# Taps in DRAM by lag then row, a modulation chunk in another place, and eight final stores of 32 rows

## The chip, the cores and the metric

The kernel runs on one core of a Trainium2 chip. The metric is the device time of one execution in microseconds (us), the median of several runs. The engines are PE (TensorE: matmuls; its weight loads are listed as PEld), DVE (VectorE), ACT (ScalarE), POOL (GpSimd) and SP (SyncE, which here only issues DMAs). DMAs are issued from the queues of SP, ACT and POOL and are carried by 16 DMA engines.

## What is computed

Two layers of a diffusion backbone over 256 latent tokens and 256 context tokens, width 1024. Layer 0 mixes tokens with a bidirectional diagonal state space (S5, 64 groups of 16 channels, 64 states per group) and a gated linear unit (GLU), then a dense SwiGLU. Layer 1 is grouped-query attention and a top-2-of-8 expert SwiGLU. Every sub-layer is modulated by vectors that come from one wide product:

```python
def _modulation(cvec, w, b):
    return jnp.split(jax.nn.silu(cvec) @ w + b, N_MOD, axis=-1)     # w: (1024, 6 * 1024) per layer

def _s5_mixer(hl, hc, ...):
    for r in range(2):                                              # forward, reverse
        sc_re, sc_im = _s5_scan(u_c, ..., None, reverse)            # context
        fin = last state of the context
        sl_re, sl_im = _s5_scan(u_l, ..., fin, reverse)             # latent, starts from it
        y_l = y_l + _s5_readout(sl_re, sl_im, c_re[r], c_im[r])
        y_c = y_c + _s5_readout(sc_re, sc_im, c_re[r], c_im[r])
    ...
# layer:  xl = xl + ml[2] * mixer(...);  xl = xl + ml[5] * ffn(...)
```

The output is the latent stream, 256 x 1024 float32.

## The kernel before

**State space part.** The 512 tokens are cut into 64 blocks of 8 tokens (32 context, 32 latent). Within a block the state space is a short convolution whose kernel (the *taps*: 15 lags, -7 to 7, a 16 x 16 matrix for each of the 64 groups) is worked out on the chip; between blocks a recurrence over 63 steps carries the states (*the scan*, `scan_range`, three DVE instructions a step, lines 844, 847, 849).

**Main loop.** 18 rounds (`for i in range(n + 2)`), three stages deep: `z_mul` (products on DVE, line 574, in some rounds sums, line 579), `z_tr` (transposes on PE, line 588, evicted by ACT, line 589), `v_stage` (PE lines 654 and 655) and `t_stage` (PE line 667, evicted by ACT into `VS`, lines 670 and 673). Work of `w_gen` (DVE, lines 680 to 702) fills gaps. At the end of the loop the order of DVE, ACT and PE is pinned to the order in which the code is written.

**Modulation chunks.** `ada_todo` is a list of 20 chunks of 512 columns, (0,4) to (0,11) and then (1,0) to (1,11), always taken in that order. For a chunk, two loads of 1 MB go out on SP; `ada_go` does 16 matmuls (line 264) and an eviction (line 270); `ada_done` does four transposes (line 284) and an eviction into `part` (line 285). With the last chunk of a group, which is (0,11), (1,3) or (1,11), two DVE instructions follow that sum `part` into `cols` (lines 289 and 291). Before the change the chunks go like this: (0,4) to (0,10) in the seven rounds named by `FILL`; (0,11) and (1,0), named `two`, within the taps, after `taps(1)` and after `taps(2)`; (1,1) and (1,2) after the two halves of the context read-out; and (1,3) in the `while` behind it, which runs until 8 are left. Loads use a rotation of four 1 MB buffers, `raw`.

**Taps and windows.** `taps(q)`, q from 0 to 3, works out a quarter of the taps on PE (lines 771 and 776) with ACT building the weights (line 755), and writes it to a DRAM tensor `Kd` by six DMAs on SP (lines 782 to 784). `windows(blk, hf)` reads a quarter back as a block Toeplitz matrix, 128 rows x 2048 values, 1 MB, on SP (line 791): row (a, l) of it holds the taps of lags a to a + 7 for channel l. `inner` multiplies it with the tokens (PE line 804) into eight `pz` banks. Then `states` copies scan states (ACT line 858; line 875 is the place of its call that the trace names), `outer` multiplies them in (PE line 866), and `gelu` evicts. The context half (h = 0) needs scan steps 1 to 31; the latent half (h = 1) needs all of them and follows the end of the scan. After it the GLU starts (PE line 1027).

In the stretch of the taps, the order of ACT, PE and SP is pinned to the written order. The order of DVE is not: there the tile planner, which works with costs of its own, decides where the two instructions of a `cols` sum stand among the scan's.

**End.** After the last expert, `finish` adds its result to `acc` in four DVE instructions (line 1992), and `store` sends each quarter of the output (128 rows of tokens, half of the columns) to DRAM on SP (line 2048).

Of the kernel before, what the change touches and what calls it, by code (L numbers as in the profile page):

```python
# [10 lines left out]
F32 = mybir.dt.float32  # L11
# [11 lines left out]
G, P, I = 64, 64, 16  # L23
# [20 lines left out]
AT = (15, 6, 4, 6, 6, 7, 25, 26, 26, 26, 28, 28, 29, 29, 29, 29, 30, 30, 33, 33, 33, 33, 34, 35, 35, 35, 35, 35, 35, 36)  # L44
RAW3 = 2
WOP = ((13, 13, 17, 17, 18, 19, 20, 20, 21, 21, 22, 22, 24, 24, 24, 24), (29, 29, 30, 30, 31, 32, 33, 34, 35, 35, 36, 36))
FILL = (3, 5, 6, 7, 10, 11, 13)
LATE = 8
ZSUM = (4, 5, 6, 8, 10, 13, 15)
WN = (0, 6, 1, 2, 1, 1, 2, 2, 2, 2, 1, 4, 2, 1)  # L50
# [29 lines left out]
def backbone_kernel(ctx: ExitStack, tc: tile.TileContext, x, c, cx, c_ctx, ada_w, ada_b, norm_mix_g, norm_ffn_g,  # L80
# [212 lines left out]
    def ada_next(n):  # L293
        return [ada_load(*ada_todo.pop(0)) for _ in range(min(n, len(ada_todo)))]
# [9 lines left out]
    def ada_done():  # L304
        while ada_open:
            ada_turn(*ada_open.pop(0))
# [17 lines left out]
    for r in range(2):  # L324
        src = bn[:, r].rearrange("g r (p i) -> g (r p) i", i=I)
        for q in range(2):
            t = ps()
# [269 lines left out]
    t = ps()  # L597
    T.transpose(t[:, :128], pr, ident)
    S.activation(pcol, t[:, :128], AF.Copy)
    t = ps()  # L600
# [141 lines left out]
        pass  # L742


    Kd = dram.tile([4, I, 15, 16 * I], F32, name="Kd")
    bd = [[wk.tile([128, 4, 64], F32, name=f"bd{r}{b}") for r in range(2)] for b in range(2)]
    for b in range(2):
        for r in range(2):
# [2 lines left out]
    def bd_fill(n_):  # L751
        for r in range(2):
            for d in range(2):
                rs = slice(64 * d, 64 * d + 64)
                S.activation(bd[n_ % 2][r][rs, :, 16 * d:48].rearrange("p g (o i) -> p g o i", i=16)[:, :, 0:3 - d:2 - d, :],
                             BB[r][rs, 4 * n_:4 * n_ + 4, None, :].to_broadcast([64, 4, 2, 16]), AF.Copy)

    def taps(q):

        ks = wk.tile([128, 9, 8, I], F32, name="ks", bufs=2)  # L760
        for q4 in range(4):
            n_ = 4 * q + q4
            if n_ + 1 < 16:
                bd_fill(n_ + 1)
            t = ps()
            tv = t[:, :288].rearrange("p (g s i) -> p g s i", g=2, s=9)
            for j in range(2):
                for r in range(2):
                    for zz in range(2):
                        gl = 2 * j + zz  # L770
                        T.matmul(t[64 * zz:64 * zz + 64, 144 * j:144 * j + 144], lhsT=bd[n_ % 2][r][:, gl, :],  # L771
                                 rhs=W[q // 2][r][:, (4 * n_ + gl) % 32].rearrange("p s i -> p (s i)"),
                                 start=(r == 0), stop=False)
                for zz in range(2):
                    rs = slice(64 * zz + 32, 64 * zz + 48)
                    T.matmul(t[64 * zz:64 * zz + 64, 144 * j:144 * j + 16], lhsT=ident[rs, 64 * zz:64 * zz + 64],
                             rhs=dm[rs, 2 * n_ + j, :], start=False, stop=True)
            S.activation(ks[:, :, 2 * q4:2 * q4 + 2, :].rearrange("p s g i -> p g s i"), tv, AF.Copy)
        for zz in range(2):
            kv = Kd[q, :, :, 128 * zz:128 * zz + 128]  # L780
            k_ = ks.rearrange("p s g i -> p s (g i)")
            SY.dma_start(kv[:, 8:15], k_[64 * zz:64 * zz + 16, 1:8])
            SY.dma_start(kv[:, 0:7], k_[64 * zz + 16:64 * zz + 32, 2:9])
            SY.dma_start(kv[:, 7], k_[64 * zz + 32:64 * zz + 48, 0])
# [3 lines left out]
    def windows(blk, hf):  # L788
        M = Mt[blk, hf] = raw_tile([8, 16 * I])
        k_ = Kd[2 * blk + hf]  # L790
        SY.dma_start(M.rearrange("p t k -> p (t k)"),
                     bass.AP(tensor=k_.tensor, offset=k_.offset, ap=[[16 * I, 8], [15 * 16 * I, 16], [1, 8 * 16 * I]]))

    def outs(pz, hf):
        for b in range(4):
# [9 lines left out]
                     start=(gl < 4), stop=False)  # L805

    two = [ada_next(1)[0] for _ in range(2)]
    bd_fill(0)
    pz = {}
    for q in range(4):  # L810
        taps(q)
        if q == 1:
            for hf in range(2):
                windows(0, hf)
            ada_done()
            ada_go(two[0])
        elif q == 2:
            ada_done()
            ada_go(two[1])
    for hf in range(2):  # L820
        windows(1, hf)
    ada_done()
# [1220 lines left out]

    ov = out[0].rearrange("(c b t) d -> b t c d", b=2, t=4)

    def store(lt, n):
        ns = slice(512 * n, 512 * n + 512)
        SY.dma_start(ov[lt, :, :, ns], acc[:, lt, ns])

    def finish():  # L2050

        e_ = NE - 1
        y = mp.tile([128, 512], F32, name="y0", tag="y0")
        for n in range(2):
            rs_n = slice(64 * n, 64 * n + 64)
            V.tensor_tensor(y[rs_n, :], yps[e_][0][rs_n, :], grow[0][rs_n, 512 * n:512 * n + 512], op=OP.mult)
        for lt, n, t in spread(e_, y):
            add(e_, lt, n, t)
            store(lt, n)

    def chain(*gens):
        for g in gens:
# [52 lines left out]
    with tc.If(nmax > 128):  # L2115
        op_, op_cm = popen("op", 1, "right")
        for e_ in range(NE):
            se = op_.tile([128, 2, 128], F32, name="se")
            pz = op_.tile([128, 2], F32, name="pz")
            V.tensor_scalar(pz, pos[:, :, e_], capv[:, e_:e_ + 1], None, op0=OP.subtract)  # L2120
            hf = op_.tile([128, 2, D], F32, name="hf")
            for lt in range(2):
                V.tensor_scalar(se[:, lt, :], iota, pz[:, lt:lt + 1], None, op0=OP.is_equal)
                V.tensor_tensor(hf[:, lt, :], h2[0][:, lt, :].bitcast(F32), h2[1][:, lt, :].bitcast(F32), op=OP.add)
            xg = op_.tile([128, KT, 128], F32, name="xg")
            for q in range(2):
                t = ps()
                for j in range(4):
                    for lt in range(2):
                        T.matmul(t[:, 128 * j:128 * j + 128],  # L2130
                                 lhsT=hf[:, lt, 512 * q + 128 * j:512 * q + 128 * j + 128], rhs=se[:, lt, :],
                                 start=(lt == 0), stop=(lt == 1))
                S.activation(xg[:, 4 * q:4 * q + 4, :].rearrange("p a b -> p (a b)"), t, AF.Copy)
            yp = [ps("py") for _ in range(2)]
            for f in range(DFF // 256):
                t = ps()
                for half in range(2):
                    w = load(moe_gu[0, e_].rearrange("(k p) n -> p k n", p=128)[:, :, DFF * half + 256 * f:
                                                                                  DFF * half + 256 * f + 256], [KT, 256])
                    for kt in range(KT):  # L2140
                        T.matmul(t[:, 256 * half:256 * half + 256], lhsT=xg[:, kt, :], rhs=w[:, kt, :],
                                 start=(kt == 0), stop=(kt == KT - 1))
                a = op_.tile([128, 256], F32, name="a")
                S.activation(a, t[:, 0:256], AF.Silu)
                V.tensor_tensor(a, a, t[:, 256:512], op=OP.mult)
                t = ps()
                for j in range(2):
                    T.transpose(t[:, 128 * j:128 * j + 128], a[:, 128 * j:128 * j + 128], ident)
                aT = op_.tile([128, 256], F32, name="aT")
                S.activation(aT, t[:, 0:256], AF.Copy)  # L2150
                w = load(moe_dn[0, e_][256 * f:256 * f + 256, :].rearrange("(k p) n -> p k n", p=128), [2, D])
                for j in range(2):
                    for n in range(2):
                        T.matmul(yp[n], lhsT=aT[:, 128 * j:128 * j + 128], rhs=w[:, j, 512 * n:512 * n + 512],
                                 start=(f == 0 and j == 0), stop=(f == DFF // 256 - 1 and j == 1))
            so = op_.tile([128, 256], F32, name="so")
            t = ps()
            for lt in range(2):
                T.transpose(t[:, 128 * lt:128 * lt + 128], se[:, lt, :], ident)
            S.activation(so, t[:, 0:256], AF.Copy)  # L2160
            for n in range(2):
                y, u = [op_.tile([128, 512], F32, name=t_) for t_ in ("y", "u")]
                S.activation(y, yp[n], AF.Copy)
                for lt in range(2):
                    t = ps()
                    T.matmul(t, lhsT=so[:, 128 * lt:128 * lt + 128], rhs=y, start=True, stop=True)
                    av = acc[:, lt, 512 * n:512 * n + 512]
                    V.scalar_tensor_tensor(u, t, gates[:, lt, e_:e_ + 1], grow[0][:, 512 * n:512 * n + 512], op0=OP.mult, op1=OP.mult)
                    V.tensor_tensor(av, av, u, op=OP.add)
        for n in range(2):  # L2170
            for lt in range(2):
                store(lt, n)
        pclose(op_cm)


# [28 lines left out]
```

## Time and profile before

| what | value |
|---|---|
| median of 3 runs | 1636.08 us (1635.64 to 1639.44) |
| profiled execution: its own time | 1639.6 us |
| profiled execution: span of the trace | 1637.8 us |
| PE busy | 1493.1 us (91%) |
| DVE busy | 891.7 us (54%) |
| ACT busy | 705.7 us (43%) |
| DMA queue of SP | 392.13 MB, 65.9% of 16 engines |

How to read it: the shares are means over stages with different limits. From about 940 us to the end the 16 DMA engines are full with expert weights; from about 270 to 940 us PE is nearly full; ahead of that stands the state space part, where PE, DVE and the DMA engines each have long gaps. [...] All times in the rows below are counted from the start of the span.

### The profile page before, as it was taken

The numbers are of one execution on the slowest core, as the hardware profiler recorded it, in microseconds if no ns is written. First come the engines' busy times: TensorE is split into PE (matmuls) and PEld (weight loads), VectorE is DVE, ScalarE is ACT, GpSimd is POOL, SyncE is SP. The second block draws the span as 40 slices with busy tenths as digits, with TensorE's granted clock in tenths as the row PEclk, the third lists the DMA queues.
The fourth block names the chain that finished last, engine by engine and source line by source line (L and its number), as shares of the span: only waits on it lengthen the run. The fifth ranks groups of instructions, "written<-read, shape, count | busy, mean of one in ns | idle before, by whom it ended". The sixth has DMA issues, their size and how long they took to land.

```text
span 1637.8 us, 24181 instructions
## 1 busy us (share of the span) xinstructions
PE 1493.1 (91%) x9790; PEld 1055.9 (64%) x9790; DVE 891.7 (54%) x1385; ACT 705.7 (43%) x930; POOL 38.3 (2%) x69
## 2 busy tenths in 40 slices
PE   4898656999999999999899899989999999989994
PEld 3555446876888888878767778437853685367631
DVE  6996568336333343335786777327831785168611
ACT  4687355325221221224585566226721673056400
POOL 1001000000000000001001000000000000000020
PEclk9996777999999999999999899999999999999998
DMA  9672585426332332235441579999999999999994
GB/s 264 229 261 60 108 209 171 156 81 218 107 102 77 103 103 84 97 103 158 172 164 48 205 254 360 387 403 409 405 406 402 408 405 405 404 408 405 395 405 192
DMA packets 163720, 398.48 MB, mean 243 GB/s; under 512 B 11964, under 2 KB 62336, under 8 KB 162960
## 3 DMA queue, kind: packets, MB, share of 16 engines
q1 hardware_dynamic: 161408, 392.13, 65.9%
q0 software_dynamic: 1184, 3.18, 0.8%
q10 hardware_dynamic: 1008, 1.55, 0.4%
q8 instruction: 79, 1.29, 0.3%
q14 instruction: 41, 0.34, 0.1%
HBM read 394.78 MB, written 2.05 MB: 242 GB/s over the span
## 4 chain that ended last, share of the span: by engine, by line
PE 77%; DMA 8%; DVE 5%; ACT 4%; issue 1%; SPq 0%; ACTq 0%; DVEq 0%
PE pgu L971 10%; PE pgu L970 10%; PE pgu L972 10%; PE pgu L1921 8%; DMA raw<-in_moe_w_gate_up_dram 3%; DMA raw<-Kd 3%; PE pd L970 3%; PE pd L972 3%; PE pd L971 3%; PE py L970 2%; PE py L971 2%; PE py L1984 2%; PE py L972 2%; PE ada L264 1%; PE ps L771 1%; DMA raw<-in_moe_w_down_dram 1%
## 5 line engine op out<-in xcount | busy, mean ns | idle before, releaser
L951 DVE TENSOR_TENSOR lo<-raw,hi 128x2048 fp32r<-128x2048 f32 (+1 forms) x184 | 401.1, 2187 | 215.5 <-ACT hi L951 214.6
L951 ACT ACTIVATE hi<-raw 128x2048 fp32r<-128x2048 f32 (+1 forms) x184 | 337.4, 1834 | 323.8 <-PE pd L971 81.1
L1921 PE MATMUL pgu<-raw,xb 128*32 128x512 f32 (+1 forms) x1536 | 157.0, 558 | 2.2 <-DMA raw<-in_moe_w_gate_up_dram 2.2
L970 PE MATMUL pgu<-hi,xa 128*128 128x512 f32 (+1 forms) x384 | 148.4, 386 | 5.3 <-ACT hi L951 5.3
L971 PE MATMUL pgu<-lo,xa 128*128 128x512 f32 (+1 forms) x384 | 147.2, 383 | 5.5 <-DVE lo L951 5.5
L972 PE MATMUL pgu<-hi,xa 128*128 128x512 f32 (+1 forms) x384 | 146.0, 380 | 0.0
L970 PE MATMUL pgu<-hhi,hi 128*128 128x512 f32 x352 | 137.0, 390 | 0.5 <-ACT hhi L1102 0.5
L971 PE MATMUL pgu<-hlo,hi 128*128 128x512 f32 x352 | 137.1, 390 | 0.0
L972 PE MATMUL pgu<-hhi,lo 128*128 128x512 f32 x352 | 137.0, 389 | 0.0
L1921 PEld LDWEIGHTS pgu<-raw,xb 128*32 128x32 f32 x1536 | 48.4, 110 | 98.7 <-issue 86.6
L970 PEld LDWEIGHTS pgu<-hi,xa 128*128 128x128 f32 x384 | 74.5, 194 | 23.7 <-ACT hi L951 6.0
L971 PEld LDWEIGHTS pgu<-lo,xa 128*128 128x128 f32 x384 | 74.6, 194 | 19.1 <-DVE lo L951 6.4
L1984 PE MATMUL py<-raw,aT 128*32 128x512 f32 x704 | 80.3, 594 | 6.4 <-DMA raw<-in_moe_w_down_dram 6.2
L972 PEld LDWEIGHTS pgu<-hi,xa 128*128 128x128 f32 x384 | 74.4, 194 | 13.8
L970 PEld LDWEIGHTS pgu<-hhi,hi 128*128 128x128 f32 x352 | 66.0, 188 | 15.1 <-ACT hhi L1102 1.4
L971 PEld LDWEIGHTS pgu<-hlo,hi 128*128 128x128 f32 x352 | 66.1, 188 | 14.6 <-DVE ncq L1099 0.8
L972 PEld LDWEIGHTS pgu<-hhi,lo 128*128 128x128 f32 x352 | 66.1, 188 | 13.6
L970 PE MATMUL pd<-act,hi 128*128 128x512 f32 x176 | 70.0, 399 | 0.0
L972 PE MATMUL pd<-act,lo 128*128 128x512 f32 x176 | 69.5, 395 | 0.0
L971 PE MATMUL pd<-act,hi 128*128 128x512 f32 x176 | 69.5, 395 | 0.0
L970 PE MATMUL py<-hi,aT 128*128 128x512 f32 x176 | 69.2, 393 | 0.0
L971 PE MATMUL py<-lo,aT 128*128 128x512 f32 x176 | 69.0, 392 | 0.0
(444 smaller groups left out, 2365.9 us busy)
## 6 DMA issues: line engine op xcount, KB each, us to landing
raw<-in_moe_w_gate_up_dram SPq DMA_DIRECT2D x128, 1024.0 KB
raw<-in_moe_w_down_dram SPq DMA_DIRECT2D x88, 1024.0 KB
raw<-in_ada_w_dram SPq DMA_DIRECT2D x48, 1024.0 KB
raw<-in_moe_w_gate_up_dram SPq DMA_DIRECT2D x64, 768.0 KB
raw<-in_ffn_w_gate_up_dram SPq DMA_DIRECT2D x22, 1024.0 KB
raw<-in_ssm_glu_w_dram SPq DMA_DIRECT2D x8, 1024.0 KB
raw<-in_ffn_w_down_dram SPq DMA_DIRECT2D x8, 1024.0 KB
raw<-in_attn_w_qkv_dram SPq DMA_DIRECT2D x6, 1024.0 KB
```

Source lines behind the costliest of these rows:

```text
L264: T.matmul(pt[32 * j:32 * j + 32, :], lhsT=sc32[:, 4 * h + j, :], rhs=ld_[2][h][:, j, :], start=(h == 0), stop=(h == 1))
L771: T.matmul(t[64 * zz:64 * zz + 64, 144 * j:144 * j + 144], lhsT=bd[n_ % 2][r][:, gl, :], rhs=W[q // 2][r][:, (4 * n_ + gl) % 32].rearrange ...
L951: ins = [S.activation(hi, r, AF.Copy), V.tensor_tensor(lo, r, hi.bitcast(F32), op=OP.subtract)]
L970: T.matmul(o, lhsT=a[0], rhs=b[0], start=start, stop=False)
L971: T.matmul(o, lhsT=a[0], rhs=b[1], start=False, stop=False)
L972: T.matmul(o, lhsT=a[1], rhs=b[0], start=False, stop=stop)
L1921: T.matmul(pt[64 * j_ + 32 * q:64 * j_ + 32 * q + 32, 0:bw], lhsT=XB[:, kt, o + 32 * q:o + 32 * q + 32], rhs=wj_[j_][:, kk, b:b + bw], sta ...
L1984: T.matmul(yps[e_][0][64 * n + 32 * q:64 * n + 32 * q + 32, :], lhsT=aT[1][:, m, 32 * q:32 * q + 32], rhs=wt_[0][:, kk, ns], start=first, ...
```

## The change

1. `Kd` is laid out as quarter, lag, row, values in place of quarter, row, lag, values. The writes name the same pieces through a rearranged view. The read has 128 rows outside, each of eight pieces of 256 values (1 KB); before, it had 8 outside, then 16, each of one piece of 2048 values (8 KB).
2. `FILL` names an eighth round, 9, so the main loop takes (0,4) to (0,11). `two` is then (1,0) and (1,1). `two[0]` is multiplied ahead of `taps(0)`, and transposed after it; `two[1]` is multiplied after `taps(1)` and transposed after `taps(2)`. Chunks (1,2) and (1,3) follow the two halves of the context read-out, and the `while` has nothing to do.
3. `store(lt)` sends 128 rows with all 1024 columns as four DMAs of 32 rows, by turns on the queues of SP and ACT, once both halves are added.

```diff
-FILL = (3, 5, 6, 7, 10, 11, 13)
+FILL = (3, 5, 6, 7, 9, 10, 11, 13)
...
-    Kd = dram.tile([4, I, 15, 16 * I], F32, name="Kd")
+    Kd = dram.tile([4, 15, I, 16 * I], F32, name="Kd")
...
-            kv = Kd[q, :, :, 128 * zz:128 * zz + 128]
+            kv = Kd[q, :, :, 128 * zz:128 * zz + 128].rearrange("l j k -> j l k")
...
-        SY.dma_start(M.rearrange("p t k -> p (t k)"),
-                     bass.AP(tensor=k_.tensor, offset=k_.offset, ap=[[16 * I, 8], [15 * 16 * I, 16], [1, 8 * 16 * I]]))
+        SY.dma_start(M, bass.AP(tensor=k_.tensor, offset=k_.offset, ap=[[16 * I, 128], [16 * 16 * I, 8], [1, 16 * I]]))
...
     two = [ada_next(1)[0] for _ in range(2)]
+    ada_done()
+    ada_go(two[0])
     bd_fill(0)
     pz = {}
     for q in range(4):
         taps(q)
-        if q == 1:
+        if q == 0:
+            ada_done()
+        elif q == 1:
             for hf in range(2):
                 windows(0, hf)
-            ada_done()
-            ada_go(two[0])
+            ada_go(two[1])
         elif q == 2:
             ada_done()
-            ada_go(two[1])
...
-    def store(lt, n):
-        ns = slice(512 * n, 512 * n + 512)
-        SY.dma_start(ov[lt, :, :, ns], acc[:, lt, ns])
+    def store(lt):
+        for t in range(4):
+            (SY, S)[t % 2].dma_start(ov[lt, t], acc[32 * t:32 * t + 32, lt, :])
...
             add(e_, lt, n, t)
-            store(lt, n)
+            if n:
+                store(lt)
```

## Rows read from the trace of the kernel before

**Rows 1.** Chain of waits, 120 to 285 us: start, length (us), what it was.

```profile
192.12 2.24 DMA Kd<-ks
194.57 25.86 DMA raw<-Kd
...
264.25 1.19 ACT sx L858 x2
```

**Rows 2.** Timeline of DVE, 156 to 245 us: start, length, instruction, [idle before <- releaser].

```profile
158.22 0.42 DVE L844 TENSOR_TENSOR sq<-VS,T 128x256 f32<-128x256 f32 x1
...
178.09 0.42 DVE L289 TENSOR_REDUCE cols<-part 128x64 f32<-128x256 f32 x1 [17.23 <-ACT part L285]
...
179.08 0.42 DVE L844 TENSOR_TENSOR sq<-VS,T 128x256 f32<-128x256 f32 x1
...
180.19 0.43 DVE L844 TENSOR_TENSOR sq<-VS,T 128x256 f32<-128x256 f32 x1
...
242.97 0.29 DVE L289 TENSOR_REDUCE cols<-part 128x32 f32<-128x128 f32 x1 [10.44 <-ACT part L285]
```

**Rows 3.** Busy time by stretch: engines (x instructions), PE clock, DMA share, GB/s.

```profile
150.00:160.00 10.00, 10.00 (x82) 7.12 (x80) 9.86 (x13) 5.31 (x17) 0.59 (x4) 0.50 0.17 25
168.00:170.00 2.00, 2.00 (x14) 0.24 (x6) 0.00 (x0) 0.00 (x0) 0.00 (x0) 0.50 0.66 94
182.00:184.00 2.00, 2.00 (x32) 1.34 (x28) 1.79 (x7) 1.85 (x7) 0.00 (x0) 1.00 0.46 106
279.00:282.00 3.00, 3.00 (x15) 2.49 (x14) 0.08 (x1) 1.78 (x1) 0.00 (x0) 1.00 1.09 349
1626.00:1628.00 2.00, 0.00 (x0) 0.00 (x0) 0.00 (x0) 0.00 (x0) 0.00 (x0) 0.50 0.28 102
```

**Rows 4.** Timeline at the main loop's end, 121 to 137 us, several engines.

```profile
121.83 1.29 DVE L579 TENSOR_TENSOR zq<-zq,zq 128x512 f32<-128x512 f32 x2
...
123.47 1.92 PE L264 MATMUL ada<-raw,sc 128*32 128x512 f32 x16
...
126.02 0.60 ACT L270 ACTIVATE R<-ada 128x512 f32<-128x512 f32 x1
...
126.69 0.64 PE L284 MATMUL cp<-kc,R 128*128 128x128 f32 x4
...
127.94 0.23 ACT L285 ACTIVATE part<-cp 128x32 f32<-128x32 f32 x1
...
128.76 1.04 PE L588 MATMUL ps<-kc,zq 128*128 128x128 f32 x8
...
136.10 1.23 DVE L698 TENSOR_TENSOR W<-PQ,CD 128x1024 f32<-128x1024 f32 x1 [1.44 <-PE ps L667]
```

**Rows 5.** Timeline of PE and ACT, 142 to 240 us.

```profile
142.41 1.41 PE L771 MATMUL ps<-W,bd 128*64 128x144 f32 x8 [6.41 <-ACT bd L755]
...
166.39 3.64 PE L264 MATMUL ada<-raw,sc 128*32 128x512 f32 x16
...
187.32 1.95 PE L804 MATMUL pz<-raw,U 128*32 128x128 f32 x64
...
209.13 1.96 ACT L858 ACTIVATE sx<-VS 64x992 f32<-64x992 f32 x1 [21.51 <-DVE VS L849]
...
220.57 3.64 PE L804 MATMUL pz<-raw,U 128*32 128x128 f32 x64 [9.19 <-DMA raw<-Kd]
...
239.46 0.20 ACT L285 ACTIVATE part<-cp 128x32 f32<-128x32 f32 x1 [0.74 <-PE cp L284]
```

**Rows 6.** Timeline of SP's DMA issues, 187 to 196 us.

```profile
190.35 0.30 SPq L783 DMA_DIRECT2D Kd<-ks  x1
...
193.35 1.80 SPq L791 DMA_DIRECT2D raw<-Kd  x2
```

**Rows 7.** Timeline of the end, from 1618 us.

```profile
1619.17 2.79 DVE L1992 SCALAR_TENSOR_TENSOR acc<-ps,gater,acc 128x512 f32<-128x512 f32 x4 [0.56 <-PE ps L2000]
...
1619.95 3.25 SPq L2048 DMA_DIRECT2D out_dram<-acc  x4
```

More of the change, by code (lines that the diff above doesn't have):

```diff
@@ L2169, in backbone_kernel @@
                     V.tensor_tensor(av, av, u, op=OP.add)
-        for n in range(2):
-            for lt in range(2):
-                store(lt, n)
+        for lt in range(2):
+            store(lt)
         pclose(op_cm)
```

## The prediction

> **What bounds the kernel now.** The view by stretch comes first. From 940 us on the DMA engines are full and from 270 to 940 us PE is, and the change touches neither but for the last stores. Whatever it moves ahead of 270 us shifts all that follows, since every later load waits for a buffer that earlier work frees. So two places count: 120 to 270 us, and the end.
>
> For the first, read the chain of waits, then DVE's timeline. The chain names the window read (25.86 us ending at 220.43) and then, from 242.97, only DVE's scan, up to the state copy at 264.25 [rows 1, 2]. The scan is a chain of 62 steps of 1.11 us (179.08 to 180.19), later shorter, started at 158.22 [rows 2]. DVE stood still in it twice, 17.23 and 10.44 us, in front of two `cols` sums that waited for ACT's `part`, with the rest of the scan queued behind them [rows 2]. Without the two waits the scan would have ended 27.7 us earlier; the window read holds the end up only because the second sum hangs on what follows it.
>
> At the end DVE is done at 1619.17 + 2.79 = 1621.96, and then only stores run, at 102 GB/s with 0.28 of the DMA engines [rows 3, 7]: some four of 16, as many as the store's outermost dimension.
>
> **Main loop: later by 4.7 us.** The eighth chunk costs PE 1.92 + 0.64 us and ACT 0.60 + 0.23 [rows 4]. Bounds are 0 (all beside other work) and 2.6; I take 2.0, near PE's end, since the chunk stands in PE's pinned order between two stages. Its two loads go onto SP ahead of those for the next chunks; SP there only waits for buffers, and two chunks are in flight, so I cost them at nothing; if a load came late, each us would count in full.
>
> The change also adds a wait. The eighth chunk of the loop is now (0,11), whose `cols` sum stands in DVE's pinned order between `z_mul(14)` and `z_mul(15)`. Before, DVE was through `z_mul(15)` by 121.83 + 1.29 = 123.1, long ahead of its transposes at 128.76 [rows 4]. Now it must wait for `part`, 127.94 + 0.23 + 2.0 = 130.2, then do the sum (0.42 us from the row of the first sum, 0.6 with its addition) and five products of 0.65: 134.0 [rows 2, 4]. The transposes, due at 130.8, can start with the first operand done, about 133.5: 2.7 us lost, behind which PE's and ACT's last rounds are queued. DVE's next work waited for PE's last `t_stage` at 136.1 [rows 4], so it shifts by the sum, 4.7 us. Bounds: 0 and 5.8.
>
> **First wait of the scan: gone.** Then the first sum isn't in the scan. It begins at 158.22 + 4.7 = 162.9. From 158.22 to 264.25 are 106.0 us; less 17.23, less 10.44, less the sum's 0.6 leaves 77.8: with no wait at all the scan would end at 240.7.
>
> **Taps.** `two[0]` is multiplied in PE's idle 6.41 us ahead of the taps [rows 5], so its 16 matmuls are hidden; its eviction, 0.6, stands on ACT ahead of the first weights. If that gap closed, up to 3.64 us would show. Taps start at 142.41 + 4.7 + 0.6 = 147.7. `taps(0)` and `taps(1)` took 24.0 (142.41 to 166.39), at clock 0.50 [rows 3, 5]; transposes of `two[0]` between them 1.3 at that clock; `two[1]` behind them 3.64. Before, 170.03 to 187.32 held two taps, one chunk and two sets of transposes; less 1.92 and 0.64 that is 14.7. So taps end at 191.3, 4.0 us later than before.
>
> **Windows.** SP's writes of the last quarter stopped until 190.35, when the first windows had landed; from there to the next window issue passed 3.0 us [rows 6]. With windows that land early the stop is gone: issue at 191.3 + 0.3 + 3.0 = 194.6. The old read ran on half of the engines, 0.46 at 106 GB/s, with 8 outside [rows 3]. No row shows the new shape. Nearest is the weight read in the GLU, also 128 rows outside and 1 KB pieces: 349 GB/s, 1.09 of the engines [rows 3]. I take that, 3.0 us per MB; the other end is the old rate. With 2.24 us for a landing (the write of 8 KB [rows 1]) the windows are there at 199.8 and 202.8; before, the second came at 220.4. PE then needs 3.64 for each (half clock, as at 220.57 [rows 5]), to 207.1, where it was 224.2: 17.1 earlier. State copies are ready sooner: the first at 209.13 - 17.23 - 0.6 + 4.7 = 196.0, two of them for PE's first `outer`, 199.9 [rows 5]. The writes to `Kd` keep count and size; I cost their new pitch at nothing, within 1 us.
>
> **Second wait: shorter.** Only two chunks follow the windows now, so the `part` that ended a group is where that of (1,2) was, 239.66 [rows 5], less 17.1: 222.6. Where the sum stands in the scan, the planner chooses. Before, it stood 57.1 us of DVE work into the scan (242.97 less 158.22 and both waits). With one chunk less (242.97 - 239.66 = 3.3) and without the first sum I put it at 53.2, step 49. DVE gets there at 162.9 + 53.2 = 216.1 and waits 6.5 us. The scan ends at 240.7 + 6.5 = 247.2, which is **17.0 us** earlier than 264.25. The GLU's loads have buffers by then. The `while` chunk that is gone stood beside the scan; its worth is in this wait already.
>
> **Stores.** Before, 1 MB at 102 GB/s took 10.3 us from about the first issue, 1619.95 [rows 3, 7]. Now the last four stores leave at 1622.0 to 1622.9, two on each queue, 2.95 us later than that first issue, with at most half of the data to go. 32 rows outside aren't in the trace; 16 rows outside (`Kd` writes of 512 B) held 0.66 of the engines [rows 3], more than 8 or 4 did. At 25.5 GB/s per engine and 16 engines I allow 0.7 us for the rest: 10.3 - 2.95 - 0.7 = **6.7 us**. Bounds: 4.2 (half rate), 7.3, and 0 if they don't spread. ACT is idle there, so its two issues cost nothing. [...]
>
> **Sum.** 17.0 + 6.7 = 23.7. The profiled execution took 1639.6 (span 1637.8), 3.5 over the median of 1636.08; it would take 1615.9, and the median becomes **1612.4**.
>
> **Rivals.**
> (A) *The second sum stands earlier.* If the planner puts it at step 40, 43.3 us into the scan, 34.5 us of scan follow 222.6: end at 257.1, gain 7.2 + 6.7, **1622.2**. For it: the planner was 17 and then 27.7 us too early before. Against: the same planner and the same chain put it at step 52. 0.14.
> (B) *The read isn't faster*: re-reading one small stretch of DRAM holds it, not the number of engines. 2 MB at 106 GB/s land at 216.6, PE is through at 220.2, `part` at 235.7, and 24.6 us of scan follow: 260.3, **1625.5**. Against: 0.46 of the engines looks like eight of 16. 0.08.
> (C) *The clock is up in the taps.* [...] Against: PE still idles some 5 us after the chunk, and 24 us of dense taps at 0.50 (10.00 busy in 150 to 160 us) did not raise it [rows 3]. [...] 0.10.
> (D) *Stores don't spread*: **1619.1**. 0.04.
> (E) *Slower*: the eight-fold overlap read in 1 KB pieces collapses in DRAM. The scan ends 44.4 us after the last window. To be 4.9 us slower than before it must land after 231.5, so 2 MB in 34.7 us, 60 GB/s; the old pair managed 84 with loads beside it. At 40 GB/s it gives **1658.8**. 0.03. A rate around 65 gives no change, 0.03 together with all else that would cancel out.
>
> **How the numbers follow.** The forecast has 0.58; its own unknowns (loop 0 to 5.8, second wait 0 to 10, stores 4.2 to 7.3) spread it over 1601 to 1619. The range 1601 to 1623 adds A, C and D: 0.86; B and E are left out. A measurement of this kernel tells 0.3%, 4.9 us, from no change. All but E and the last case are beyond it on the fast side: faster 0.93, same 0.04, slower 0.03.
>
> **What would show it.** Right: two `raw<-Kd` waits of a few us at most; DVE's timeline with no gap in the first 40 steps and one of 3 to 10 us near step 49; a DVE gap of some 7 us ahead of `z_mul(15)`; the main loop's end 4 to 5 us later; the GLU's start 17 us earlier; DMA share near 1 in the last stores and under 4 us of them. Wrong: `raw<-Kd` still at half of the engines, a sum far ahead of step 49, the clock at 1.00 in `taps(0)`, or expert stages that start 17 us earlier and don't end so.

## The result and the profile after

The changed kernel takes **1611.38 us** (median of 4 runs, 1610.32 to 1613.94) against 1637.19 (4 runs, 1635.64 to 1639.44) of the kernel before: ratio 0.9844, 95% interval 0.9826 to 0.9861. The forecast was 1612.4, range 1601 to 1623. The profiled execution took 1610.32, with a span of 1608.5; it is the fastest of the four, while the profiled execution of the kernel before (1639.44, span 1637.8) is the slowest of its four, so the spans differ by more than the medians.

The chain of waits of the changed kernel, 120 to 285 us (start, length, what it was), no longer holds any window read. The chain of the kernel before had two, 44.81 us together: the 25.86 of [rows 1] and this one.

```profile
171.39 18.95 DMA raw<-Kd
```

The chain after (line numbers have shifted by one: L803 was L804, L845 was L844):

```profile
130.90 0.43 DVE cols L289
131.57 1.81 DVE zq L574 x3
...
196.95 2.00 ACT sx L859
...
222.12 0.29 DVE cols L289
...
244.21 1.19 ACT sx L859 x2
```

DVE's timeline of the same execution (start, length, instruction, idle before it and its releaser), against [rows 2 and 4]:

```profile
130.90 0.42 DVE L289 TENSOR_REDUCE cols<-part 128x64 f32<-128x256 f32 x1 [8.93 <-ACT part L285]
141.45 1.23 DVE L698 TENSOR_TENSOR W<-PQ,CD 128x1024 f32<-128x1024 f32 x1 [1.23 <-PE ps L667]
163.57 0.41 DVE L845 TENSOR_TENSOR sq<-VS,T 128x256 f32<-128x256 f32 x1
222.12 0.29 DVE L289 TENSOR_REDUCE cols<-part 128x32 f32<-128x128 f32 x1 [2.55 <-ACT part L285]
```

The first sum now stands in the main loop, whose end came 5.35 us later (141.45 for 136.10). Of the scan's two waits, 17.23 and 10.44, one of 2.55 is left. PE and ACT around the windows:

```profile
148.46 1.42 PE L771 MATMUL ps<-W,bd 128*64 128x144 f32 x8 [5.25 <-ACT bd L755]
169.53 1.92 PE L264 MATMUL ada<-raw,sc 128*32 128x512 f32 x16
185.98 3.70 PE L803 MATMUL pz<-raw,U 128*32 128x128 f32 x128
195.47 4.97 PE L803 MATMUL pz<-raw,U 128*32 128x128 f32 x128 [5.79 <-DMA raw<-Kd]
201.08 1.96 PE L867 MATMUL pz<-W,sx 128*32 128x128 f32 x64 [0.63 <-ACT sx L876]
205.07 1.96 PE L867 MATMUL pz<-W,sx 128*32 128x128 f32 x64 [2.04 <-ACT sx L876]
207.01 1.91 ACT L876 ACTIVATE sx<-VS 64x992 f32<-64x992 f32 x1
208.94 1.28 ACT L872 ACT_TABLE_LOAD   x1
210.23 0.60 ACT L872 ACTIVATE Z<-pz 128x512 f32<-128x512 f32 x1
210.88 2.80 PE L264 MATMUL ada<-raw,sc 128*32 128x512 f32 x16 [3.86 <-ACT Z L872]
```

The taps end at 185.98 and the second windows are there at 195.47; then PE waits for ACT, not for a DMA. Busy time by stretch (length, PE, PEld, DVE, ACT, POOL, each with its instructions, PE clock as the granted share of full speed, DMA share, GB/s), in a window read and in the last stores:

```profile
176.00:180.00 4.00, 4.00 (x54) 2.84 (x54) 3.62 (x12) 3.73 (x12) 0.00 (x0) 1.00 1.05 355
1598.00:1600.00 2.00, 0.00 (x0) 0.00 (x0) 0.71 (x2) 0.00 (x0) 0.00 (x0) 1.00 0.88 209
1600.00:1602.00 2.00, 0.00 (x0) 0.00 (x0) 0.00 (x0) 0.00 (x0) 0.00 (x0) 0.75 0.96 277
```

That is 355 GB/s at a share of 1.05 for 106 at 0.46, and in the stores 277 at 0.96 for 102 at 0.28 [rows 3]. In the stores each busy engine moves no more than before, 18 GB/s (277 / 16 / 0.96) for 23 (102 / 16 / 0.28), so the gain there is in the number of engines at work.

**Where the 29.3 us between the two spans went.** The span falls into four parts, cut at the chunk of round 13 of the main loop (PE L264), the GLU's first matmul and the first of `finish`'s four last additions (us; the columns of the experiments are used below):

| kernel | round-13 chunk at | from there to the GLU | GLU to last additions | from there to the end |
|---|---|---|---|---|
| before | 123.47 | 147.25 | 1348.5 | 18.63 |
| after | 126.20 | 124.49 | 1345.2 | 12.58 |
| chunk_alone | 126.27 | 150.76 | 1346.2 | 18.64 |
| windows_alone | 125.02 | 143.11 | 1346.0 | 18.69 |
| stores_alone | 124.08 | 147.54 | 1348.4 | 11.48 |
| without_windows | 127.54 | 152.88 | 1345.6 | 12.37 |
| read_by_16_rows | 125.51 | 129.01 | 1347.9 | 10.32 |
| lag_by_16_rows | 125.42 | 128.65 | 1358.2 | 11.21 |
| stepped_16_rows | 125.70 | 128.99 | 1346.9 | 10.77 |
| late_sums | 127.25 | 119.17 | 1346.7 | 11.83 |
| sums_no_chunk | 125.03 | 119.19 | 1346.5 | 12.58 |
| warm_taps | 126.04 | 123.06 | 1347.4 | 12.02 |
| stores_on_sp | 127.98 | 127.25 | 1347.0 | 11.70 |

Before to after: +2.73, -22.76, -3.2 and -6.05. The third part holds nothing of the change, and over the other kernels it lies between 1345.6 and 1348.4 (1358.2 apart, see the end), so the -3.2 is put down to that spread, which no run tests. The other three make 26.1; the medians differ by 25.8.

### The profile page after: what moved, and what is told of

Its sections match the earlier page's. It is cut to its first block, busy times and chain, and to the rows that moved or that the text cites. A ratio compares the mean times of both kernels' runs of the same rounds, so it can differ in the third digit from the quotient of the medians.

```text
span 1608.5 us, 24184 instructions
## 1 busy us (share of the span) xinstructions
PE 1485.4 (92%) x9790; PEld 1051.1 (65%) x9790; DVE 891.8 (55%) x1385; ACT 706.2 (44%) x930; POOL 38.5 (2%) x69
## 4 chain that ended last, share of the span: by engine, by line
PE 77%; DVE 8%; DMA 5%; ACT 4%; issue 1%; SPq 0%; DVEq 0%; ACTq 0%
PE pgu L972 10%; PE pgu L971 10%; PE pgu L973 10%; PE pgu L1922 8%; DMA raw<-in_moe_w_gate_up_dram 3%; PE pd L971 3%; PE pd L972 3%; PE pd L973 3%; PE py L972 3%; PE py L971 3%; PE py L1985 2%; PE py L973 2%; DVE sq L845 1%; DMA raw<-in_moe_w_down_dram 1%; PE ada L264 1%
```

## The experiments

**One part at a time.** chunk_alone has `FILL` with the eighth round and the new order of `two`; windows_alone only the new `Kd` and its read; stores_alone only the eight stores; without_windows is the change with the old `Kd` and read. The diffs below show the main lines of each; `...` stands for lines not shown.

```diff
# chunk_alone
-FILL = (3, 5, 6, 7, 10, 11, 13)
+FILL = (3, 5, 6, 7, 9, 10, 11, 13)
...
+    ada_done()
+    ada_go(two[0])
     bd_fill(0)
...
# windows_alone
-    Kd = dram.tile([4, I, 15, 16 * I], F32, name="Kd")
+    Kd = dram.tile([4, 15, I, 16 * I], F32, name="Kd")
...
+        SY.dma_start(M, bass.AP(tensor=k_.tensor, offset=k_.offset, ap=[[16 * I, 128], [16 * 16 * I, 8], [1, 16 * I]]))
...
# stores_alone
+        for t in range(4):
+            (SY, S)[t % 2].dma_start(ov[lt, t], acc[32 * t:32 * t + 32, lt, :])
...
```

> The chunk is moved (eighth FILL round, the first of the two ahead of the taps), the window read and the stores are as before. Theory (scan with its waits): the first wait of 17.2 us goes, but the main loop ends 5.4 us later and the second sum still waits for what follows the old window reads: they land about 223 us, the sum is ready about 239 to 242 us, and some 24.6 us of scan follow, so the GLU starts at 270 to 274 us (before: 271.5) and the time is within -2 to +4 us of before. Rival (each removed wait is worth its length): GLU at 260 us, -12 us (17.2 gained, 5.4 lost).

> Only the layout of the taps in DRAM and the window read are changed. Theory: the windows land about 195 us in place of 220 us, yet the first wait of 17.2 us in the scan stays, so step 31 and the state copies come at 209 us as before, the matmuls with the states start at about 213 us in place of 224 us, the second sum is ready at 232 to 235 us, where the scan arrives anyway; GLU start 261 to 264 us, time -7 to -10 us. Rival (the window read is the bound, the scan is hidden by it): GLU at 250 us, -20 us or more. Rival (re-reading one stretch of DRAM holds the read): windows as late as before, 0 us.

> Only the eight final stores of 32 rows. Theory: from the first of the last four additions to the end 12.6 us in place of 18.6, so -6 us, with the DMA engines nearly full in the stores (share near 0.9) and nothing else moved. Rival (the changed kernel's shorter end came from its earlier stages, for instance emptier queues): less than -3 us.

> The changed kernel with the old layout and the old window read: chunk and stores together. Theory: the sum of the chunk alone (-2 to +4) and the stores (-6): -8 to -2 us against before, so the window read is worth 18 to 24 us once the first wait is gone, though 7 to 10 us alone. Rival (parts add up independently): the chunk's part would be -20 + 8.5 = -11.5, and this kernel -17.5 us.

| kernel | median us | median of before beside it | ratio, 95% interval |
|---|---|---|---|
| chunk_alone | 1641.32 | 1639.03 | 1.0032 (1.0003 to 1.0060) |
| windows_alone | 1633.70 | 1639.03 | 0.9973 (0.9950 to 0.9996) |
| stores_alone | 1631.07 | 1639.03 | 0.9956 (0.9936 to 0.9977) |
| without_windows | 1638.91 | 1639.03 | 1.0005 (0.9977 to 1.0033) |

The three parts alone bring +2.3, -5.3 and -8.0 us, 11 together; the whole brings 25.8. The rest comes from two of them, the chunk and the windows, being there at once. DVE's timeline of chunk_alone (first fence) and the timelines of windows_alone (second fence) show how:

```profile
248.47 0.29 DVE L289 TENSOR_REDUCE cols<-part 128x32 f32<-128x128 f32 x1 [27.46 <-ACT part L285]
```

```profile
179.84 0.42 DVE L289 TENSOR_REDUCE cols<-part 128x64 f32<-128x256 f32 x1 [17.45 <-ACT part L285]
...
210.89 1.92 ACT L857 ACTIVATE sx<-VS 64x992 f32<-64x992 f32 x1 [21.52 <-DVE VS L848]
...
214.87 3.64 PE L865 MATMUL pz<-W,sx 128*32 128x128 f32 x64 [10.69 <-ACT sx L874]
...
240.43 0.29 DVE L289 TENSOR_REDUCE cols<-part 128x32 f32<-128x128 f32 x1 [6.14 <-ACT part L285]
```

With the chunk alone the first wait is gone, and DVE stands 17.0 us longer in the second: its `part` still hangs on the late window read (the last windows are waited for until 230.30). What the first wait gives, the second takes, and the loop's delay is left. I had expected the last windows at 223 and the GLU at 270 to 274 us; it came at 277.03.

With the windows alone the first wait stays, 17.45, and the second only falls from 10.44 to 6.14: PE has the windows early, but then waits 10.69 us for the state copies, which need scan step 31, and the scan is held up by the first wait until 179.84. The mechanism is the one expected, but the sum was ready at 240.4, not at 232 to 235, the GLU started at 268.13, not at 261 to 264, and the gain was 5.3 us, not 7 to 10.

So the scan's end is the later of two paths, DVE's own steps and the windows with the sum behind them. Each edit shortens one of them. In without_windows the second wait is 29.56, the GLU starts 9.7 us later than before (280.42 for 270.72), and the new stores' 6 us pay for most of that; I had expected a gain of 2 to 8 us, and it was 0.1. stores_alone gained 8.0 for the 6 expected.

All thirteen profiles bear this out: from the first step of the scan to the GLU (which starts at the sum of the first two columns of the table), less DVE's waits for the sums in between, it is always 84.4 to 84.8 us (before 112.50 less 27.67, after 87.12 less 2.55, without_windows 114.13 less 29.56, and 84.42 in late_sums below, which has no wait). So the scan and its waits set the start of the GLU, and the windows act on it through the second wait alone.

**Both sums out of the way.** late_sums is the changed kernel with the first sum behind the products of `z_mul(15)` and the second in the GLU, behind the scan:

```diff
+            if i == n - 1:
+                hold.clear()
+                ada_sum()
             z_tr(i)
...
-    pin((VE, SE_, TE))
+    last = pin((VE, SE_, TE))
+    hold.clear()
+    ada_sum()
+    queue({VE: last[VE]})
```

> The changed kernel with both sums of DVE moved out of the way: the sum for chunk (0,11) after the products of round 15, the one for (1,3) into the GLU. Theory (DVE is the bound from 131 us to the GLU): the idle time ahead of the products of round 15 is gone and PE does not wait for them (2.5 us), the scan has no wait and no sum (2.55 + 0.5 us): GLU start at 245 to 247 us when the round-13 chunk starts at 126.2 us, so 5 to 6 us less than the changed kernel. Rival (state copies or PE follow closely): 0 to -2 us.

1607.30 us against 1638.88, ratio 0.9807 (0.9786 to 0.9828). From the chunk to the GLU it takes 119.17, which is 5.32 less than after. Of that 2.6 are the loop (first sum's wait 5.09, hidden beside PE's last rounds) and 2.55 the second wait. DVE's timeline of late_sums:

```profile
131.99 0.42 DVE L298 TENSOR_REDUCE cols<-part 128x64 f32<-128x256 f32 x1 [5.09 <-ACT part L287]
139.89 1.23 DVE L707 TENSOR_TENSOR W<-PQ,CD 128x1024 f32<-128x1024 f32 x1 [1.43 <-PE ps L676]
254.70 0.28 DVE L298 TENSOR_REDUCE cols<-part 128x32 f32<-128x128 f32 x1
```

From the chunk the loop ends 12.64 us on (139.89 less 127.25), after 15.25 (141.45 less 126.20). So the wait that the change adds to the loop, and the wait that it leaves in the scan, both go, each seen in its own stretch, and the scan runs without a gap.

sums_no_chunk asks whether the chunk's move is then still worth its place: the windows and stores of the change, the old `FILL` and order of `two`, and both sums in the GLU (the second one's parts lie in a 64 KB table that is loaded again behind it).

```diff
+    hold[:] = [1]
...
+    ada_sum()
+    queue({VE: last[VE]})
+    GP.dma_start(kc[:, 256:384], kconst[:, 256:384])
```

> The windows and the stores of the change, and the modulation chunk left in the taps; both column sums stand behind the scan, in the GLU, so that VectorE waits for neither. (The second sum's parts lie in a table that is loaded again behind it, one DMA of 64 KB.) Theory one, the chunk's move only serves to bring the first sum's parts early: with the sums out of the scan it buys nothing and costs its place in the main loop, so leaving it out saves the 2.0 to 2.7 us of its matmuls in round 9 against late_sums: 1604.5 to 1605.5 us, and the scan has no gap. Theory two, the move also brings the windows and the inner products early enough: without it the windows land 4 us later and the last outer products end behind the scan, 1608 us or more. Theory three, neither: within 1 us of late_sums' 1607.3.

1604.62 us against 1637.34, ratio 0.9806 (0.9776 to 0.9836). From the chunk to the GLU it is 119.19, as in late_sums, and the chunk of round 13 starts 2.2 us earlier. So once no sum stands in the scan, the move buys nothing in the trace and costs its place in the loop, as theory one had it; the two ratios don't tell the kernels apart. Both medians lie some 4 to 7 us under that of the changed kernel. The interval of late_sums just touches that of the changed kernel (0.9826 to 0.9861) and that of sums_no_chunk overlaps it, so the gain rests on the traces, where the stretch from the chunk to the GLU is 5.3 us shorter in both.

**How the read became faster.** read_by_16_rows keeps the old `Kd` and reads each window in eight DMAs of 16 rows; lag_by_16_rows does the same in the new layout; stepped_16_rows differs from that only in the rows of one DMA, which lie 8 partitions apart:

```diff
 for a in range(8):
-    SY.dma_start(M[16 * a:16 * a + 16],
-                 bass.AP(tensor=k_.tensor, offset=k_.offset + 16 * 16 * I * a, ap=[[16 * I, 16], [16 * 16 * I, 8], [1, 16 * I]]))
+    SY.dma_start(M[a:128:8],
+                 bass.AP(tensor=k_.tensor, offset=k_.offset + 16 * I * a, ap=[[8 * 16 * I, 16], [16 * 16 * I, 8], [1, 16 * I]]))
```

> The changed kernel, but with the old layout of the taps, and each window read as eight DMAs of 16 rows with the old pieces of 8 KB. It tells the number of rows outside from the size of the pieces. Theory (the number outside sets how many DMA engines work): DMA share near 1 in the reads, the last window there 2 to 6 us later than in the changed kernel (eight issues of 0.45 us for one), GLU start 249 to 257 us, time -20 to -27 us against before. Rival (long pieces, or re-reading one stretch of DRAM, hold the rate at 106 GB/s): last window after 215 us, GLU start near 270 to 281 us, time about that of the kernel without the window change.

> The changed kernel with its layout by lag, and each window read in eight DMAs of 16 partitions (pieces of 1 KB) in place of one of 128 rows. The run read_by_16_rows, with the old layout and pieces of 8 KB, filled all 16 engines (share 1.06) and yet moved only about 150 GB/s, so that having 16 engines at work is not the whole of it. Theory one, the layout by lag and its pieces set the rate of an engine: share about 1.0 and 340 to 370 GB/s here too, the second pair of windows lands some 6 to 8 us after its issue, and the time is that of the changed kernel, 1611 us within 3. Theory two, a DMA of 16 rows, which gives each engine one row, is slow in itself: about 150 GB/s at a share near 1.0, the second pair lands about 10 to 15 us after its issue, the second sum comes some 10 us later, and the time is that of read_by_16_rows, 1617 us within 3.

> lag_by_16_rows with one thing changed: each of the eight DMAs of a window writes 16 rows that lie 8 partitions apart (0, 8, 16 ...) in place of 16 neighbouring ones. Count of DMAs, rows in a DMA, size of the pieces and layout in DRAM are the same. Theory one, a DMA of 16 rows is slow since each engine has but one row to move: 126 to 155 GB/s again with the engines full, second windows 10 us after their issue, the time that of lag_by_16_rows. Theory two, the 16 neighbouring partitions are what holds it, whatever the engines: the rate at least doubles towards the 350 GB/s of the DMA of 128 rows, 250 to 350 GB/s, the second windows land 6 to 8 us after their issue, and the time is some 5 us or more below that of lag_by_16_rows. [...]

Busy time by stretch in the first window reads of read_by_16_rows, lag_by_16_rows and stepped_16_rows, and for the last SP's issue of these reads:

```profile
178.00:186.00 8.00, 8.00 (x124) 5.99 (x128) 7.25 (x23) 6.07 (x19) 0.00 (x0) 1.00 1.04 149
```

```profile
178.00:188.00 10.00, 9.20 (x164) 6.92 (x162) 9.08 (x27) 5.97 (x19) 0.00 (x0) 1.00 1.18 129
```

```profile
178.00:182.00 4.00, 4.00 (x56) 2.96 (x52) 3.62 (x12) 3.56 (x12) 0.00 (x0) 1.00 0.67 195
```

```profile
172.91 10.66 SPq L792 DMA_DIRECT2D raw<-Kd  x16
```

With 16 neighbouring rows all 16 engines are busy (shares 1.18 and 1.04) and yet move 129 to 149 GB/s, with 8 KB pieces and with 1 KB pieces alike. So neither the number of engines nor the layout is the whole of it. With rows 8 partitions apart the engines are busy for 0.67 of the time and move 195 for 129, half as much again; no run shows the double that I had expected. That is the rate at which SP issues, since 16 DMAs of 128 KB in 10.66 us are 197 GB/s. For each busy engine it is 18 GB/s (195 / 16 / 0.67) in place of 7 (129 / 16 / 1.18). So 16 neighbouring rows in a DMA are a cause of their own, and the one DMA of 128 rows is free of it. The step also spreads the rows of a DMA in DRAM, from 1 KB to 8 KB apart, and no run changes the one without the other; but in read_by_16_rows they lie 15 KB apart in DRAM, and it was slow all the same, which speaks for the partitions. Why 16 neighbouring rows are slow is in no trace here. Whether the same held the old read, at 14 GB/s for each of its eight engines (106 / 16 / 0.46) where the new one has 21 (355 / 16 / 1.05), was not tried.

The times of these three (1616.77 against 1638.88, ratio 0.9862; 1625.01 against 1637.34, 0.9907; 1617.07 against 1638.88, 0.9863) say nothing of the read. In these three, with eight DMAs for a window in the code, the planner put the second sum behind 62 steps, and on ACT a state copy ahead of its `part`, which waits for a scan step until 228.5 to 228.7. ACT's timeline of stepped_16_rows:

```profile
218.63 0.60 ACT L270 ACTIVATE R<-ada 128x512 f32<-128x512 f32 x1
228.74 1.93 ACT L861 ACTIVATE sx<-VS 64x1024 f32<-64x1024 f32 x1 [9.52 <-DVE VS L852]
...
235.21 0.20 ACT L285 ACTIVATE part<-cp 128x32 f32<-128x32 f32 x1 [1.21 <-PE cp L284]
```

DVE then waits 6.5 to 6.8 us for that sum in all three, and from the round-13 chunk to the GLU they agree within 0.4 us, though stepped_16_rows has its second windows 5 us sooner than lag_by_16_rows (PE goes on with them at 200.32 for 205.32). So read_by_16_rows gained the 22 us that I had expected, but not by way of the read, and my expectation for the other two, that the time would follow the read, failed: the place of the sum and of the copy decided.

**The clock in the taps.** warm_taps does the chunk's 16 matmuls three times ahead of the taps:

```diff
+    warm = wk.tile([128, 1], F32, name="warm")
     ada_done()
     ada_go(two[0])
+    for _ in range(2):
+        pt = ada_mm(two[0])
+        S.activation(warm[:, 0:1], pt[:, 0:1], AF.Copy)
```

> The changed kernel with the 16 matmuls of the chunk ahead of the taps done three times (3.8 us more of PE work in PE's idle stretch before the taps, results of the two extra ones unused but for one column). Theory (the clock falls to 0.50 because PE idles there, and after that the windows no longer bound the end): the clock stays at 1.00 through the first two taps, these take 14 to 16 us in place of 21 to 24, yet the GLU starts no more than 3 us earlier, because the state copies after step 31 hold the matmuls. Rival (PE and the windows still bound the stretch): the GLU starts 5 to 10 us earlier. Rival on the clock (it falls anyhow): taps at 24 us.

1609.62 us against 1638.88, ratio 0.9816 (0.9791 to 0.9842), not to be told from the changed kernel. The 48 matmuls ran at full clock (1.00), and it fell all the same, to 0.53. Busy time by stretch of warm_taps:

```profile
142.00:148.00 6.00, 5.70 (x52) 1.62 (x50) 5.40 (x5) 5.94 (x11) 0.30 (x2) 1.00 0.01 3
148.00:150.00 2.00, 0.12 (x2) 0.12 (x4) 1.97 (x3) 1.90 (x8) 0.00 (x0) 1.00 0.00 0
150.00:160.00 10.00, 9.80 (x80) 6.73 (x80) 10.00 (x9) 5.83 (x19) 0.00 (x0) 0.53 0.01 2
```

Behind them PE waits two us for ACT's weights, and from 150 to 160 us the taps run at a clock of 0.53, before at 0.50 [rows 3]. The experiment did not keep the clock up, so it does not test what that would bring. It shows something else: here the planner put the second sum behind 55 steps, where DVE does not wait for it at all, and from the chunk to the GLU it is 123.06 for 124.49.

**Two queues or one for the stores.** stores_on_sp issues all eight on SP:

```diff
-            (SY, S)[t % 2].dma_start(ov[lt, t], acc[32 * t:32 * t + 32, lt, :])
+            SY.dma_start(ov[lt, t], acc[32 * t:32 * t + 32, lt, :])
```

> The changed kernel with all eight stores on SP. Theory (the number of rows outside gives the gain, the second queue only issue time): from the first of the last four additions to the end 13 to 14 us (12.6 in the changed kernel, 18.6 before), time within 1.5 us of the changed kernel; the stretch of the taps as in the changed kernel, so it also shows whether the clock rises in the second taps again. Rival (two queues share the work): 15 us or more.

1613.13 us against 1638.88, ratio 0.9830 (0.9802 to 0.9858). SP needs 5.20 us for the eight where each queue needed 2.54 and 2.57 for four, and the end comes 11.70 after the first addition (after 12.58). I had expected 13 to 14 on one queue. The second queue buys nothing that shows; the 32 rows outside do it. The median lies 1.75 us over the changed kernel's, a little more than the 1.5 that I allowed; the profile shows one reason.

Up to the stores this is the changed kernel, so it is also a second look at the scan, and here PE's clock did not rise until the chunk behind `taps(1)` (0.50 from 160 to 172 us and from 176 to 180 us). PE's and DVE's timelines of stores_on_sp:

```profile
176.68 3.64 PE L264 MATMUL ada<-raw,sc 128*32 128x512 f32 x16
194.85 3.70 PE L803 MATMUL pz<-raw,U 128*32 128x128 f32 x128
226.69 0.28 DVE L289 TENSOR_REDUCE cols<-part 128x32 f32<-128x128 f32 x1 [3.90 <-ACT part L285]
```

From the round-13 chunk the taps end 7.1 us later than in the profile of after (66.87 for 59.78), and the second wait is 1.35 longer. The loop, some of it at the lower clock (0.83 from 130 to 140 us, after 1.00), adds 1.43. The two, 2.78, make the 2.76 by which the GLU is later.

## Why the prediction was right, and where it was right by chance

| step | predicted | measured |
|---|---|---|
| chunk in the loop | 2.0 | 2.73; over all profiles 2.0 (126.43, mean of nine with it, less 124.40, mean of four without) |
| DVE's wait ahead of `z_mul(15)` | 2.7 | 2.64 (transposes at 134.13, for 128.76 + 2.73) |
| start of the scan | 162.9 | 163.57 |
| start and end of the taps | 147.7, 191.3 | 148.46, 185.98 |
| rate of the window read | 349 GB/s | 355 |
| second windows at PE | 199.8 | 195.47 |
| PE through the windows | 207.1 | 200.44 (195.47 + 4.97) |
| second sum ready | 222.6 | 222.1 |
| second sum in the scan, wait | step 49, 6.5 | behind 50 steps, 2.55 |
| GLU earlier by | 17.0 | 20.0 |
| stores | 6.7 | 6.05; over all profiles 7.0 (18.65, mean of three, less 11.69, mean of ten) |

The mechanism was right: two waits, one gone and one short, and the read off the path. Three terms were off; that two of them cancelled is luck.

*The taps ended 5.3 us earlier than forecast.* I had the clock rise behind the chunk that follows `taps(1)`, as before. In this execution it rose within `taps(1)`, at 164 (0.50 from 160 to 164 us, 1.00 from 164 to 168), and the chunk ran at full clock (1.92 for 3.64). That is rival C, the clock up in the taps, by half.

*And the sum was ready no earlier, because ACT became the bound.* I took the 15.5 us from PE's last window matmul to `part` from the kernel before, where the last of the six state copies was done at 220.70, before PE came to them. Timeline of ACT and PE before:

```profile
218.79 1.91 ACT L875 ACTIVATE sx<-VS 64x992 f32<-64x992 f32 x1
...
223.95 4.32 PE L866 MATMUL pz<-W,sx 128*32 128x128 f32 x128
```

Now they run from 196.95 to 208.9, one behind the other, `gelu` stands behind them on ACT (Z at 210.2), and PE waits for both, 0.63, 2.04 and 3.86 us. From 200.44 to 222.1 are 21.7 us. I had rival C at 1605.9 us, 6.5 under the forecast, with the copies as the next bound; the 7.1 us between this profile and that of stores_on_sp were worth 1.35. It was priced too high, since ACT's copies and `gelu` come next.

*The second wait was mis-sized, 6.5 for 2.55.* The planner moved the sum by one step (50 for 51), not by the 3.3 us that I took off, so DVE came at 219.57 rather than 216.1. The wait is 3.95 us shorter; the scan started 0.67 later and took 0.3 more without its wait, which leaves the 3.0 us by which the GLU came earlier than forecast. Where the planner puts the sum I only guessed from the kernel before. In the experiments it stands behind 50, 51, 55 or 62 steps, so that its place came out within two steps of the forecast is in part luck too.

The 0.65 lost on the stores is within their spread. The 0.7 us allowed there for the rest of the data fits a quarter of the 1 MB at 16 times 25.5 GB/s (102 / 4, [rows 3]); the half that the text names would take 1.3, and the sum would have been 6.05. With 3.0 us more at the GLU and 0.65 less at the end the forecast of 23.7 becomes some 26, for the 25.8 measured. The shares of 0.28 with 4 rows outermost and 0.96 with 32 go with the number of rows outermost, as forecast; SP and ACT issued four stores each within 2.54 and 2.57 us, and the data moved at 277 GB/s.

## What to carry to other kernels

Where two instructions of one engine each wait in one long chain, as the sums did here (17.23 and 10.44 us) with the rest of the scan behind them, removing one wait is worth little or nothing while the other path is as late: test the edits together before dropping either, and first ask whether the waiting instructions need to stand in the chain at all. By the traces, moving the two sums behind it brought more than moving what they wait for (GLU at 244.22 in sums_no_chunk, 250.69 after the change). For a read like this one let one DMA span all 128 rows, which gave 355 GB/s at a share of 1.05; filling the engines with DMAs of 16 neighbouring rows gave 129 to 149 GB/s at a share over 1.

## What the runs showed that was not expected

- A share of DMA engines near 1 is no proof of a good rate: 129 GB/s at 1.18 and 355 at 1.05 in the same window reads of two kernels that differ in how a read is cut.
- The clock in one and the same row of taps, which all began at 0.50 or little above (0.50 in after, 0.53 in warm_taps), rose inside `taps(1)` in five of the nine profiles that have the chunk ahead of them (in that of after at 164 us, and the next chunk's 16 matmuls took 1.92 us), and only behind the next chunk in four (3.64 us for them in that of stores_on_sp). In the four profiles without that chunk it never rose before the next one (3.64 us for its 16 matmuls in each). What decides it is open.
- In lag_by_16_rows the clock stood at 0.50 for 23 us in the attention of layer 1, where it was 0.98 in the profile of after, and the part behind the GLU is 10 to 13 us longer than in all others. Its time says so little of its window read for this reason too.

```profile
809.00:832.00 23.00, 23.00 (x102) 15.33 (x99) 9.91 (x34) 11.05 (x23) 1.26 (x2) 0.50 0.20 70
```

```profile
805.00:828.00 23.00, 23.00 (x165) 15.52 (x166) 18.79 (x55) 18.62 (x37) 1.45 (x2) 0.98 0.40 137
```

(The first is lag_by_16_rows, the second the changed kernel.)
